# The branch for tokens without a slot, moved from the middle of expert 3 into the routing, with the sums set to zero by GpSimd beforehand

## The chip, the cores and the metric

The kernel runs on one NeuronCore of a Trainium2 chip. The metric is the time of one execution in microseconds of the device (us), the median of several runs. The engines are TensorE (PE for matmuls, PEld for its weight loads), VectorE (DVE), ScalarE (ACT), GpSimd (POOL) and SyncE (SP), which here issues every load of weights.

## The reference, cut to what matters

Two decoder layers on 256 tokens of width 1024, all in float32. The second layer ends in a mixture of experts, and that part is all this study speaks of:

```python
logits = xt @ router_w + router_b            # 256 tokens x 8 experts
top_logit, top_idx = lax.top_k(logits, 2)
gates = softmax(top_logit)
out = swiglu(rows of each expert, w_gate[e], w_up[e], w_down[e])   # 1024 -> 3584 -> 1024
y = segment_sum(out[dest] * gates, tok_sorted)
x = x + gt_f * rmsnorm(y, ffn_post_g)
```

Every token is computed by two of the eight experts. The weights of all eight are read: 3 x 1024 x 3584 float32 numbers for each, 336 transfers of 1 MB in all.

## The kernel before, in words

**Routing.** `to_router` and `first_one` compute the logits, choose two experts for each token (`choose`), rank the tokens within an expert (`ranks`) and put the experts in an order by their counts (`places`, which writes the numbers of the experts to `cnt[1:9]`). The place in that order sets how many slots an expert has: `CAPS = (128, 64) * 4`. Experts at places 0, 2, 4 and 6 have 128 slots and are here called wide, those at 1, 3, 5 and 7 have 64 and are called narrow.

**Weights.** SP reads the expert's number from `cnt` and issues the loads (`load`, line 161), each into a tile of 1 MB called `raw`. The tiles come from pools listed in `turns` (12 tiles) and, for the first loads, from a longer list `first` that also borrows tiles which are needed for something else later: `yp` (1, later the sums `y`), `htp` (2), `xp` and one more. A load waits until what its tile held has been used. For a wide expert ACT and DVE split each tile into `hi` and `lo` (lines 172 and 174) and TensorE multiplies three times (lines 226, 227, 230); for a narrow one TensorE reads the tile itself (lines 1386 and 1438).

**The steps of an expert.** Seven tiles of 512 hidden columns, each with four loads of gate and up weights (`up`) and two of down weights (`down`). One-hot matrices (`onehot`, tile `disp`, line 1180 for the first expert) gather the tokens of an expert into `xT` (matmuls of line 1190, then `fl` by lines 1199 and 1201, then line 1211), and at an expert's end `scatter` adds its output to `y`. For expert 0 ACT copies the product to `y` instead (`fresh`), since `y` holds nothing yet.

**The branch.** A token for which its expert has no slot left is handled in `experts(P)`, a second pass inside `tc.If(over > S)`, called from `overflow`. With the inputs of this study the branch is not taken. `overflow` stands in the pipeline at `cut`, after the first tile of expert 3 (`OVER = 3`). Ahead of it SP issues ten loads (line 1529); then every engine reads `cnt[0]` (line 1531), compares, and jumps over the body (line 1538). `rest` computes `cnt[0]` and the counts beyond the slots three steps into expert 0.

**Order.** `order(...)` switches between regions in which the named engines keep the order of the code and regions in which a scheduler chooses. In the routing all four engines keep the code's order.

Of the kernel before, what the change touches and what calls it, by code (L numbers as in the profile page):

```python
# [17 lines left out]
P = 128  # L18
# [14 lines left out]

HX, OVER = 2, 3
AHEAD = 2
# [48 lines left out]
def kernel(ctx: ExitStack, tc: tile.TileContext, a: dict):  # L84
# [55 lines left out]
    def where(src):  # L140
        return src() if callable(src) else src
# [750 lines left out]
    def warm(n):  # L892

        for _ in range(n):
            T.matmul(psr["warm"], ident, con[:, :512], start=True, stop=True)
# [91 lines left out]
    def moe(l):  # L987
        with ExitStack() as s:
# [8 lines left out]
            some = [htp] * 2 + [lambda: xp.tile([P, UN], F, name="raw", tag="hT2")]  # L997
            first = turns + [yp] + some + [lambda: hTp.tile([P, UN], F, name="raw", tag="hT1")]
            ring.update(n=0, slots=turns, first=first + (turns + [yp] + some) * RND + (turns + some) * RND2)
            gax = ep.tile([P, 2, NE], F, name="gax")  # L1000
# [22 lines left out]
            def places():  # L1023

                room = sqp.tile([P, D], F, name="places", tag="k4", bufs=2)
                match = room[:, :64].rearrange("p (a b) -> p a b", a=NE)
                place = room[:, 128:256].rearrange("p (k a b) -> p k a b", k=2, a=NE)
                number = room[:, 256:320].rearrange("p (a b) -> p a b", a=NE)
                kind = room[:, 64:80].rearrange("p (a b) -> p a b", a=2)
                key = room[:, 512:520]  # L1030
                cps = tr_t("counts").rearrange("p a b -> p (a b)")
                for b in range(2):
                    T.matmul(cps[:, :NE], ones, sel[:, b], start=b == 0, stop=b == 1)
                V.tensor_copy(count, cps[:, :NE])
                V.scalar_tensor_tensor(key, count, float(NE), cn("iota")[:, :NE], op0=OP.mult, op1=OP.add)
                V.tensor_tensor(match, key[:, :, None].to_broadcast(bc), key[:, None, :].to_broadcast(bc), op=OP.is_gt)
                V.tensor_reduce(nth, match, axis=X, op=OP.add)
                V.tensor_tensor(match, cn("nth")[:, :, None].to_broadcast(bc), nth[:, None, :].to_broadcast(bc),
                                op=OP.is_equal)
                V.tensor_tensor(number, match, cn("iota")[:, None, :NE].to_broadcast(bc), op=OP.mult)  # L1040
                V.tensor_reduce(key, number, axis=X, op=OP.add)
                V.tensor_copy(cnt[:, 1:1 + NE], key)

                V.tensor_scalar(kind, sel, -2.0 * S, 2.0 * S, op0=OP.mult, op1=OP.add)
                V.tensor_add(kind, kind, rank)
                for b in range(2):
                    V.tensor_tensor(place[:, b], kind[:, b, None, :].to_broadcast(bc), match, op=OP.mult)
                V.tensor_reduce(at[:, 0:2], place, axis=X, op=OP.add)
# [22 lines left out]

            def rest():

# [6 lines left out]
                V.tensor_copy(cnt[:, 1 + NE:], key)  # L1080
                V.tensor_reduce(m[:, 0:1], key, axis=X, op=OP.max)
                V.tensor_copy(cnt[:, 0:1], m[:, 0:1])
                V.tensor_tensor(beyond, rank, cap[:, None, :].to_broadcast([P, 2, NE]), op=OP.subtract)

            def pipeline(steps, before, late, cut):

                w, later, rest = {}, {}, []
                for i in range(-AHEAD, len(steps)):
# [5 lines left out]
                    if i == len(steps) - 1:  # L1094
                        order(ALL)
                    if i == cut:
                        overflow([src for src, *_ in steps[i + AHEAD - 1:]])
                    if i == -AHEAD:
                        before()
                    if i == 1 - AHEAD:  # L1100
                        more.pop()()
                    for k in range(i + AHEAD - (i == cut), min(i + AHEAD + (i != cut - 1), len(steps))):
                        if steps[k][3]:
# [5 lines left out]
                        else:  # L1109
                            raw = load(steps[k][0])  # L1110
                            w[k] = [part(raw, 0)]
                            rest.append(lambda raw=raw, w=w[k]: w.append(part(raw, 1)))
                    if i == cut:
                        for fn in rest:
                            fn()
                        rest.clear()
                    for fn in later.pop(i, []):
# [24 lines left out]
            def dispatch(es, base):  # L1142
# [77 lines left out]
                def first_one():  # L1220

                    copied, factor = psr["turned"]
                    for g in range(2):
                        copied(g, (A.copy, V.tensor_copy)[g])
                    factor()
                    logits(1)
                    warm(1)
                    choose(1)
                    ranks(1)
                    places()  # L1230
                    warm(1)
# [39 lines left out]

            def scatter(acc, ohT, gs, fresh):

# [6 lines left out]
                def add(b):  # L1280
                    for n in range(2):
                        sp = tr_t("scp").rearrange("p a b -> p (a b)")
                        for j in range(2):
# [4 lines left out]
                            else:  # L1288
                                T.matmul(sp, fr(ohT[:, b, :]), fr(eo[j][:, n, :]), start=j == 0, stop=j == 1)  # L1289
                        if fresh and b == n == 0:  # L1290
                            y.append(yp.tile([P, 2, D], F, name="y", tag="raw"))
                        yy = y[0][:, b, n * 512:(n + 1) * 512]
                        if fresh:
                            A.copy(yy, sp)
                        else:
                            V.tensor_add(yy, yy, sp)

# [42 lines left out]
            def experts(base):  # L1340
# [102 lines left out]
                def spread(e):  # L1443
                    for fn in scatter(st["acc"][e], *st["disp"][e][1](), e == base == 0):
                        yield fn()
# [23 lines left out]
                for n in range(len(tiles) + 1):  # L1469
# [25 lines left out]
                    if n:  # L1495
                        e, i = tiles[n - 1]
                        for u in range(2):
                            follow = []
                            if i == NT - 1 and u == 1 and e < NE - 1:
# [5 lines left out]
                                 small_)  # L1505
                        if (e, i) == (OVER, 0):
                            cut = len(steps)
                steps[-10][2].insert(0, (1, lambda: sums(0)))
                steps[-5][2].insert(0, (2, lambda: sums(1)))
                steps[-30][2].insert(0, (1, ending))  # L1510

                def begin():
                    todo, first_one = start(0)
                    more.append(first_one())
                    steps[0][2].extend([(1, weights), (2, todo[-1]), (3, rest)])

                pipeline(steps, begin, LATE, cut)
                order(ALL)
                finish(st["acc"][NE - 1], *st["disp"][NE - 1][1]())

            def overflow(srcs):

                region.close()
                ready = []
                while len(ready) < min(RAW + RAW2 + 1, len(srcs)):
                    pool = slot()
                    if pool is not rawp3:
                        ready.append(raw_tile(pool))
                        SY.dma_start(ready[-1], where(srcs[len(ready) - 1]))
                n = ring["n"]  # L1530
                over = nc.values_load(cnt[0:1, 0:1], min_val=0, max_val=2 * S,
# [6 lines left out]
                with tc.If(over > S):  # L1538
                    ring.update(slots=[rawp3])
                    experts(P)  # L1540
                spill.clear()
                ring.update(n=n, slots=turns, ready=ready)
                order(ALL if CAPS[OVER] < P else SET)

# [15 lines left out]

            last, gt, y, ht, more = [], [], [], [], []

# [195 lines left out]
```

## Time and profile before

| what | value |
|---|---|
| median of 3 runs | 1348.87 us (1348.35 to 1349.53) |
| the profiled execution's own time | 1351.66 us |
| its span, first to last instruction | 1349.9 us |
| mean granted TensorE clock | 0.99 |
| PE busy | 1308.9 us (97%) |
| DVE, ACT, POOL busy | 61%, 48%, 2% |
| loads of expert weights | 224 + 112 of 1 MB |

The profile divides the span into instructions of each engine, and tells for an engine's idle time which engine or transfer ended it. The experts take the stretch from about 480 us to the end. The profiled execution took 2.79 us longer than the median of the runs; a change in time is worked out within the profiled execution and applied to either.

### The profile page before, as it was taken

To read this page: it belongs to the slowest core of one execution; us is meant where nothing else is said; L and a number is where in the kernel's file an instruction comes from. 1 tells how busy PE (TensorE), PEld (TensorE's weight loads), DVE (VectorE), ACT (ScalarE), POOL (GpSimd) and SP (SyncE) were. 2 spreads that over 40 slices of the span, in tenths; PEclk is the share of its full clock that TensorE was granted. 3 is DMA by queue.
4 is the path that set the end of the run, shared out by engine and by line. 5 is a ranking of instruction groups with operands and counts; after the bars stand their busy time and mean duration, and the time that the engine had idled before them with its cause. 6 is when DMAs were issued, how large, how long until landed. Compare 5 with 4: busy or idle time off the path is not lost. (4 is left out here: it accounts for less than half of the span.)

```text
span 1349.9 us, 18673 instructions
## 1 busy us (share of the span) xinstructions
PE 1308.9 (97%) x6898; PEld 913.6 (68%) x6898; DVE 829.8 (61%) x1260; ACT 645.4 (48%) x961; POOL 27.9 (2%) x48
## 2 busy tenths in 40 slices
PE   6999999999999999999999999899999999999996
PEld 3665588888677567886567886456887556787552
DVE  4796688884688479782139884018986116987201
ACT  4553643533554357673237772027774126775101
POOL 0002000000001100000000000000000000000000
PEclk9999999999999989999999999899999999999998
DMA  9876699886710179999999999899999999999996
GB/s 376 324 276 279 228 396 341 321 319 236 308 65 17 63 314 421 421 420 391 421 421 420 421 421 402 355 421 421 421 420 421 421 420 421 420 421 417 415 396 247
DMA packets 67121, 474.52 MB, mean 352 GB/s; under 512 B 7856, under 2 KB 8272, under 8 KB 10064
## 3 DMA queue, kind: packets, MB, share of 16 engines
q1 hardware_dynamic: 67024, 473.27, 86.6%
q8 instruction: 55, 0.90, 0.3%
q14 instruction: 42, 0.34, 0.1%
HBM read 472.18 MB, written 1.06 MB: 351 GB/s over the span
## 5 line engine op out<-in xcount | busy, mean ns | idle before, releaser
L174 DVE TENSOR_TENSOR lo<-raw,hi 128x1024 fp32r<-128x1024 f32 x442 | 517.6, 1223 | 91.4 <-ACT hi L172 85.4
L172 ACT CAST hi<-raw 128x1024 fp32r<-128x1024 f32 x442 | 445.2, 1050 | 126.0 <-DMA raw<-in_moe_gu_dram 35.9
L1386 PE MATMUL egu<-raw,xT 128*64 128x256 f32 x1792 | 205.4, 384 | 2.0 <-DMA raw<-in_moe_gu_dram 2.0
L226 PE MATMUL egu<-hi,xT 128*128 128x512 f32 x448 | 179.0, 400 | 0.4 <-ACT hi L172 0.4
L227 PE MATMUL egu<-hi,xT 128*128 128x512 f32 x448 | 178.9, 399 | 0.0
L1386 PEld LDWEIGHTS egu<-raw,xT 128*64 128x64 f32 x1792 | 126.0, 138 | 72.6 <-issue 10.6
L230 PE MATMUL egu<-lo,xT 128*128 128x512 f32 x448 | 142.0, 398 | 0.9 <-DVE lo L174 0.9
L1400 DVE TENSOR_TENSOR act<-act,egu 128x512 f32<-128x512 f32 (+1 forms) x56 | 30.8, 550 | 150.8 <-PE egu L1386 150.4
L1438 PE MATMUL eacc<-raw,eT 128*64 128x512 f32 x448 | 102.3, 595 | 0.5 <-ACT eT L1415 0.5
L226 PEld LDWEIGHTS egu<-hi,xT 128*128 128x128 f32 x448 | 84.4, 188 | 25.7 <-ACT hi L172 6.0
L230 PEld LDWEIGHTS egu<-lo,xT 128*128 128x128 f32 x448 | 83.2, 188 | 22.6 <-DVE lo L174 3.8
L227 PEld LDWEIGHTS egu<-hi,xT 128*128 128x128 f32 x448 | 84.4, 188 | 19.8 <-issue 1.8
L1415 ACT COPY eT<-etp 128x256 f32<-128x256 f32 x28 | 10.4, 370 | 164.3 <-PE etp L1405 97.2
L226 PE MATMUL eacc<-hi,eT 128*128 128x512 f32 x224 | 88.8, 397 | 0.0
L227 PE MATMUL eacc<-hi,eT 128*128 128x512 f32 x224 | 88.3, 395 | 0.0
L226 PE MATMUL gu<-hi,hT 128*128 128x512 f32 (+1 forms) x192 | 72.7, 382 | 0.5 <-ACT hT L406 0.5
L227 PE MATMUL gu<-hi,hT 128*128 128x512 f32 (+1 forms) x192 | 71.5, 376 | 0.7 <-DVE hT L407 0.7
L230 PE MATMUL eacc<-lo,eT 128*128 128x512 f32 x224 | 70.7, 397 | 0.0
L226 PE MATMUL proj<-hi,hT 128*128 128x512 f32 x160 | 66.7, 419 | 2.0 <-ACT hT L447 1.0
L1397 ACT ACTIVATE act<-egu 128x512 f32<-128x512 f32 (+1 forms) x56 | 27.4, 490 | 83.9 <-PE egu L1386 82.7
L1438 PEld LDWEIGHTS eacc<-raw,eT 128*64 128x64 f32 x448 | 30.9, 137 | 52.9 <-issue 47.2
L227 PE MATMUL proj<-hi,hT 128*128 128x512 f32 x160 | 64.3, 403 | 0.0
(401 smaller groups left out, 1527.0 us busy)
## 6 DMA issues: line engine op xcount, KB each, us to landing
raw<-in_moe_gu_dram SPq DMA_DIRECT2D x224, 1024.0 KB, 18.0
raw<-in_moe_dn_dram SPq DMA_DIRECT2D x112, 1024.0 KB, 19.6
raw<-in_ada_w_dram SPq DMA_DIRECT2D x48, 1024.0 KB, 6.8
raw<-in_ffn_gu_dram SPq DMA_DIRECT2D x22, 1024.0 KB, 5.0
raw<-in_w_in_dram SPq DMA_DIRECT2D x20, 1024.0 KB, 7.0
raw<-in_ffn_dn_dram SPq DMA_DIRECT2D x11, 1024.0 KB, 5.5
raw<-in_w_out_dram SPq DMA_DIRECT2D x8, 1024.0 KB, 5.9
gate<-gate SPq DMA_DIRECT2D x3, 512.0 KB
```

What stands on the lines that cost most here:

```text
L172: A.copy(fr(hi), raw[:, i * HU:(i + 1) * HU])
L174: V.tensor_sub(fr(lo), raw[:, i * HU:(i + 1) * HU], hi)
L226: T.matmul(ps, fr(xh), fr(hi[:, o:o + n]), start=first, stop=False)
L227: T.matmul(ps, fr(xl), fr(hi[:, o:o + n]), start=False, stop=False)
L230: T.matmul(ps, fr(xh), fr(lo[:, o:o + n]), start=False, stop=last)
L1386: T.matmul(h[m][64 * n:64 * n + 64, :256], xe[:, 0, 4 * u + j, :64], w[:, j * 512 + n * 256:j * 512 + n * 256 + 256], start=u == j == 0, s ...
L1397: A.activation(h["act"], h[0][:, :h["n"]], AF.Silu)
L1400: V.tensor_mul(h["act"], h["act"], h[1][:, :h["n"]])
L1415: A.copy(h["aT"][0][:, :2, :], h["tp"][:, :2, :])
L1438: T.matmul(st["acc"][e][0][64 * n:64 * n + 64, :], h["aT"][0][:, j, 64 * u:64 * u + 64], w[:, j * D + n * 512:j * D + n * 512 + 512], star ...
```

## The change: what it does

The branch moves into the routing: `begin` now runs the rest of the routing itself, calls `overflow` right behind `places`, and only then starts the dispatch of expert 0. `cnt[0]` is computed in `places` by four short DVE instructions. `rest` becomes `without` and, with a copy of `weights`, stands inside the branch. SP issues nine loads ahead of the branch. The tile for `y` is allocated at the start and set to zero by GpSimd (a `memset` of 128x2048), so expert 0 adds to it like all the others; its pool `yp` is no longer in the list `first`.

```diff
-HX, OVER = 2, 3
+HX = 2
...
-            first = turns + [yp] + some + [lambda: hTp.tile([P, UN], F, name="raw", tag="hT1")]
-            ring.update(n=0, slots=turns, first=first + (turns + [yp] + some) * RND + (turns + some) * RND2)
+            first = turns + some + [lambda: hTp.tile([P, UN], F, name="raw", tag="hT1")]
+            ring.update(n=0, slots=turns, first=first + (turns + some) * (RND + RND2))
...
+                cap = room[:, 520:528]
+                V.tensor_scalar(cap, nth, NE / 2 - 0.5, -64.0, op0=OP.is_gt, op1=OP.mult)
+                V.scalar_tensor_tensor(cap, count, S - 64.0, cap, op0=OP.add, op1=OP.add)
+                V.tensor_reduce(m[:, 0:1], cap, axis=X, op=OP.max)
+                V.tensor_copy(cnt[:, 0:1], m[:, 0:1])
...
-                    if i == cut:
-                        overflow([src for src, *_ in steps[i + AHEAD - 1:]])
...
-                        if fresh:
-                            A.copy(yy, sp)
-                        else:
-                            V.tensor_add(yy, yy, sp)
+                        V.tensor_add(yy, yy, sp)
...
                 def begin():
+                    copied, factor = psr["turned"]
...
+                    places()
+                    overflow([src for src, *_ in steps])
+                    psr["warm"] = mm_t("warm")
                     todo, first_one = start(0)
                     more.append(first_one())
-                    steps[0][2].extend([(1, weights), (2, todo[-1]), (3, rest)])
-
-                pipeline(steps, begin, LATE, cut)
+                    steps[0][2].extend([(1, weights), (2, todo[-1])])
...
-                while len(ready) < min(RAW + RAW2 + 1, len(srcs)):
-                    pool = slot()
-                    if pool is not rawp3:
-                        ready.append(raw_tile(pool))
-                        SY.dma_start(ready[-1], where(srcs[len(ready) - 1]))
-                n = ring["n"]
+                while len(ready) < RAW + RAW2 and ring["first"][0] is not rawp3:
+                    ready.append(load(srcs[len(ready)]))
+                held, ring["first"] = ring["first"], None
...
                 with tc.If(over > S):
                     ring.update(slots=[rawp3])
+                    weights()
+                    without()
                     experts(P)
...
-            last, gt, y, ht, more = [], [], [], [], []
+            y0 = yp.tile([P, 2, D], F, name="y", tag="raw")
+            G.memset(y0, 0.0)
+            last, gt, y, ht, more = [], [], [y0], [], []
```

The program's order shows where this lands. On DVE, before, `places` ends with the reduction into `at` (line 1048) and the one-hots of expert 0 (line 1180) stand right behind it:

```order
L1041 TENSOR_REDUCE places<-places 128x8
L1042 CAST cnt<-places 128x8
L1044 TENSOR_SCALAR places<-sel 128x16
L1045 TENSOR_TENSOR places<-places,rank 128x16
L1047 TENSOR_TENSOR places<-places 128x64 x2
L1048 TENSOR_REDUCE at<-places 128x16
L1180 TENSOR_SCALAR disp<-con,at,rx 128x128 x2
```

On DVE now, at the same place, `cnt[0]` is computed (lines 1045 to 1048 of the changed kernel) and the branch (lines 1521 and 1528) closes the stretch:

```order
L1042 CAST cnt<-places 128x8
L1045 TENSOR_SCALAR places<-above 128x8
L1046 SCALAR_TENSOR_TENSOR places<-above,places 128x8
L1047 TENSOR_REDUCE m<-places 128x1
L1048 CAST cnt<-m 128x1
L1050 TENSOR_SCALAR places<-sel 128x16
L1051 TENSOR_TENSOR places<-places,rank 128x16
L1053 TENSOR_TENSOR places<-places 128x64 x2
L1054 TENSOR_REDUCE at<-places 128x16
L1521 TENSOR_LOAD cnt
L1528 COMPARE_AND_BRANCH
```

The one-hots (now line 1178) stand behind the branch's end, so four instructions and a jump came between `places` and them.

On ACT, before, the first work of expert 0 follows the copy of the transposed tokens (`xt`) directly:

```order
L924 COPY xt<-rps 128x4x128
L1201 ACTIVATE fl<-xTp,mod 128x128 x2
L1211 CAST xT<-fl 128x512
L172 CAST hi<-raw 128x1024 x2
L1201 ACTIVATE fl<-xTp,mod 128x128 x2
```

On ACT now, behind the branch, that work (now lines 1199 and 1209) begins with a load of the activation table:

```order
L1528 UNCONDITIONAL_BRANCH
L1199 ACT_TABLE_LOAD
L1199 ACTIVATE fl<-xTp,mod 128x128 x2
L1209 CAST xT<-fl 128x512
L172 CAST hi<-raw 128x1024 x2
```

One table load was added there; before, no table is loaded behind the branch.

On POOL, before, the power for the second half of the tokens (`rx`) follows that for the output norm (`qst`), and then POOL waits at the branch:

```order
L239 TENSOR_TENSOR qst<-nt,half 128x1
L239 TENSOR_TENSOR rx<-nt,half 128x1
L239 TENSOR_TENSOR qst<-nt,half 128x1
L239 TENSOR_TENSOR rx<-nt,half 128x1
L1531 TENSOR_LOAD cnt
```

On POOL now, the memset stands between the two:

```order
L239 TENSOR_TENSOR qst<-nt,half 128x1
L239 TENSOR_TENSOR rx<-nt,half 128x1
L239 TENSOR_TENSOR qst<-nt,half 128x1
L1554 MEMSET y 128x2048
L239 TENSOR_TENSOR rx<-nt,half 128x1
L1521 TENSOR_LOAD cnt
```

The power for `rx` moved behind the memset. The tile `y` lies where ACT's scratch tile `junk` lay until the routing, so the memset in its turn waits for ACT's last square (line 248).

## Rows read from the trace of the kernel before

**Rows 1.** The page: busy time of TensorE, and bytes moved in 40 equal slices.

```profile
PE 1308.9 (97%) x6898; PEld 913.6 (68%) x6898; DVE 829.8 (61%) x1260; ACT 645.4 (48%) x961; POOL 27.9 (2%) x48
...
GB/s 376 324 276 279 228 396 341 321 319 236 308 65 17 63 314 421 421 420 391 421 421 420 421 421 402 355 421 421 421 420 421 421 420 421 420 421 417 415 396 247
```

**Rows 2.** Waits of TensorE: total us, times, longest; the whole execution.

```profile
PE etp L1405 <- DVEq L1538: 4.4, 1, 4.4
...
PE egu L1386 <- DMA raw<-in_moe_gu_dram: 2.0, 1, 2.0
```

**Rows 3.** Chain that ended last, 840 to 875 us: start, us, what.

```profile
849.94 9.24 PE egu L1386 x64
...
862.98 7.06 PE egu L1386 x64
```

**Rows 4.** Instructions of lines 1531 and 1538: count, ns min/median/max, first and last start.

```profile
L1531 DVEq EVENT_SEMAPHORE  x5: 50/50/50, 841.6 to 842.0; - x5
...
L1538 SPq EVENT_SEMAPHORE  x9: 17/17/17, 850.9 to 855.2; - x9
L1538 ACTq EVENT_SEMAPHORE  x2: 17/17/17, 843.1 to 843.2; - x2
...
L1538 DVEq EVENT_SEMAPHORE  x2: 21/21/21, 849.1 to 849.2; - x2
...
L1538 ACTq COMPARE_BRANCH  x1: 50/50/50, 837.7 to 837.7; - x1
...
L1538 DVEq COMPARE_BRANCH  x1: 72/72/72, 842.8 to 842.8; - x1
```

**Rows 5.** Stretches of 5 us around the branch; last three columns: granted clock, DMA share, GB/s.

```profile
850.00:855.00 5.00, 5.00 (x28) 2.86 (x30) 0.00 (x0) 0.37 (x1) 0.00 (x0) 0.57 0.57 229
855.00:860.00 5.00, 5.00 (x46) 2.95 (x44) 0.42 (x1) 0.38 (x1) 0.00 (x0) 1.00 0.58 205
```

**Rows 6.** Timeline of the routing: start, us, instruction, idle before and releaser.

```profile
469.80 0.63 ACT L248 ACTIVATE junk<-x 128x512 f32<-128x512 f32 x1
...
472.34 0.55 POOL L239 TENSOR_TENSOR rx<-nt,half 128x1 f32<-128x1 f32 x1 [4.18 <-DVE nt L238]
...
474.15 0.23 DVE L942 SCALAR_TENSOR_TENSOR lg<-logits,rx,rbias 128x8 f32<-128x8 f32 x1 [1.89 <-PE logits L937]
...
476.87 0.17 DVE L1034 COPY above<-counts 128x8 f32<-128x8 f32 x1 [0.69 <-PE counts L1033]
477.07 0.17 DVE L1035 SCALAR_TENSOR_TENSOR places<-above,con 128x8 f32<-128x8 f32 x1
...
479.77 0.60 DVE L1180 TENSOR_SCALAR disp<-con,at,rx 128x128 f32<-128x128 f32 x2
...
480.17 6.46 PE L1190 MATMUL xTp<-disp,x 128*128 128x128 f32 x32 [1.43 <-DVE disp L1180]
```

**Rows 7.** Transfer of 4 KB while the queues were idle: KB, us to landing.

```profile
con<-in_con_dram SPq DMA_DIRECT2D x1, 4.0 KB, 1.5
```

**Rows 8.** ACT's timeline in expert 0: the table load and what follows it.

```profile
498.86 1.28 ACT L1397 ACT_TABLE_LOAD   x1
500.15 0.60 ACT L1397 ACTIVATE act<-egu 128x512 f32<-128x512 f32 x1
```

**Rows 9.** GpSimd's groups by shape: count, busy us, mean ns of one.

```profile
L1628 POOL TENSOR_TENSOR gw<-gw,con 128x1024 f32<-128x1024 f32 x1 | 3.2, 3219 | 35.5 <-DMA gw<-in_gmlp_w_dram 35.5
...
L513 POOL MEMSET xp<- 128x60 f32 x2 | 0.3, 148 | 0.9 <-ACT sc L287 0.9
...
L110 POOL MEMSET half<- 128x4 f32 x1 | 0.1, 101 | 0.3 <-POOLq L1748 0.3
```

**Rows 10.** SP's issues of loads at the end of expert 0: start, stretch of the issues, count.

```profile
575.92 12.68 SPq L161 DMA_DIRECT2D raw<-in_moe_dn_dram  x2
```

**Rows 11.** Chain that ended last, from 1295 us: start, us, what.

```profile
1300.76 3.61 PE eacc L1438 x16
...
1307.23 16.00 DMA raw<-in_moe_gu_dram
```

More of the change, by code (lines that the diff above doesn't have):

```diff
@@ L1070, in weights, with without @@
                 V.tensor_reduce(at[:, 2:6], place, axis=X, op=OP.add)
-            def rest():
+            def without():
                 room = sqp.tile([P, D], F, name="places", tag="k4", bufs=2)
@@ L1080, in rest, with pipeline @@
                 V.tensor_copy(cnt[:, 1 + NE:], key)
-                V.tensor_reduce(m[:, 0:1], key, axis=X, op=OP.max)
-                V.tensor_copy(cnt[:, 0:1], m[:, 0:1])
                 V.tensor_tensor(beyond, rank, cap[:, None, :].to_broadcast([P, 2, NE]), op=OP.subtract)
-            def pipeline(steps, before, late, cut):
+            def pipeline(steps, before, late):
                 w, later, rest = {}, {}, []
@@ L1101, in pipeline @@
                         more.pop()()
-                    for k in range(i + AHEAD - (i == cut), min(i + AHEAD + (i != cut - 1), len(steps))):
+                    for k in range(i + AHEAD, min(i + AHEAD + 1, len(steps))):
                         if steps[k][3]:
@@ L1112, in pipeline @@
                             rest.append(lambda raw=raw, w=w[k]: w.append(part(raw, 1)))
[L1113 to L1116, printed above, removed]
                     for fn in later.pop(i, []):
@@ L1220, in first_one @@
                 def first_one():
[L1222 to L1230, printed above, removed]
                     warm(1)
@@ L1270, in weigh, with scatter @@
                 V.scalar_tensor_tensor(fr(eo[1][:, n, :]), acc[n], gs, eo[0][:, n, :], op0=OP.mult, op1=OP.subtract)
-            def scatter(acc, ohT, gs, fresh):
+            def scatter(acc, ohT, gs):
                 if len(acc) == 1:
@@ L1289, in add @@
                                 T.matmul(sp, fr(ohT[:, b, :]), fr(eo[j][:, n, :]), start=j == 0, stop=j == 1)
-                        if fresh and b == n == 0:
-                            y.append(yp.tile([P, 2, D], F, name="y", tag="raw"))
                         yy = y[0][:, b, n * 512:(n + 1) * 512]
-                        if fresh:
-                            A.copy(yy, sp)
-                        else:
-                            V.tensor_add(yy, yy, sp)
+                        V.tensor_add(yy, yy, sp)
                 return [lambda: [weigh(acc, gs, eo, n) for n in range(len(acc))], lambda: add(0), lambda: add(1)]
@@ L1443, in spread @@
                 def spread(e):
-                    for fn in scatter(st["acc"][e], *st["disp"][e][1](), e == base == 0):
+                    for fn in scatter(st["acc"][e], *st["disp"][e][1]()):
                         yield fn()
@@ L1505, in experts @@
                                  small_)
-                        if (e, i) == (OVER, 0):
-                            cut = len(steps)
                 steps[-10][2].insert(0, (1, lambda: sums(0)))
@@ L1512, in begin @@
                 def begin():
+                    copied, factor = psr["turned"]
+                    for g in range(2):
+                        copied(g, (A.copy, V.tensor_copy)[g])
+                    factor()
+                    logits(1)
+                    warm(1)
+                    choose(1)
+                    ranks(1)
+                    places()
+                    overflow([src for src, *_ in steps])
+                    psr["warm"] = mm_t("warm")
                     todo, first_one = start(0)
                     more.append(first_one())
-                    steps[0][2].extend([(1, weights), (2, todo[-1]), (3, rest)])
-                pipeline(steps, begin, LATE, cut)
+                    steps[0][2].extend([(1, weights), (2, todo[-1])])
+                pipeline(steps, begin, LATE)
                 order(ALL)
@@ L1539, in overflow @@
                     ring.update(slots=[rawp3])
+                    weights()
+                    without()
                     experts(P)
                 spill.clear()
-                ring.update(n=n, slots=turns, ready=ready)
-                order(ALL if CAPS[OVER] < P else SET)
+                ring.update(n=0, slots=turns, first=held, ready=ready, last=None)
+                order(ALL)
             def free():
```

## Prediction, made before the changed kernel ran

> **What bounds the kernel now.** I read the page first. TensorE is busy for 1308.9 us of the 1349.9 us span, and from the fifteenth slice on the transfers run at 421 GB/s in nearly every slice [rows 1]. So in the experts two resources look full at once, and the question is which of them a delay is passed on by. The next view is that of TensorE's waits. In the whole execution it waits once for expert weights, for 2.0 us, and once at the branch, for 4.4 us [rows 2]. Everywhere else its next operands are there. The chain that ended last says the same: it runs through TensorE's matmuls to 1304.4 us (1300.76 + 3.61) and only then through a transfer of 16.0 us, whose tile those matmuls had just released [rows 11]. The transfers are full because they refill tiles as TensorE gives them back. At the end of expert 0 SP issues two loads 12.7 us apart, where it otherwise issues one every 2.5 us (1 MB at 421 GB/s): no tile was free [rows 10]. From the first product of expert 0 to 1304 us I therefore take TensorE as the pace, and a time lost or gained on it as lost or gained at the end.
>
> Ahead of that, in the routing, the pace is a single chain on DVE: counts, places, one-hots. TensorE sits idle for 1.43 us until the one-hots come [rows 6].
>
> **The change part by part.**
>
> *The stall in expert 3 goes.* TensorE stood still for 4.4 us there [rows 2]. [...] Removed: 4.4 + 2.2 = 6.6 us.
>
> *Transfers at the branch.* SP, once it had jumped, waited from 850.9 to 855.2 us for all the loads issued ahead to land [rows 4], so the queue ran empty: 229 and 205 GB/s in two stretches of 5 us [rows 5], a loss of 2.3 + 2.6 = 4.9 us of transfer time. The same wait comes in the routing, behind nine loads, and costs the same there. I take nothing for it in either place. In expert 0 the loads run ahead of TensorE until SP has to wait for tiles [rows 10], and 4.9 us less lead is covered by that wait. If that cover were gone, up to 4.9 us would be added.
>
> *The branch in the routing.* What stood between `places` and the one-hots was nothing; now DVE goes through these, one after another.
> - Four short instructions for `cnt[0]`, each depending on the one before. Such steps start 0.2 us apart (476.87 and 477.07) [rows 6]: 0.8 us.
> - Waits on semaphores, the load of `cnt[0]` and the comparison. In the branch of before DVE's first wait began at 841.6 us and the comparison at 842.8 us [rows 4]: 1.2 us.
> - The jump. From the comparison to the first instruction behind it, DVE took 6.3 us (842.8 to 849.1) and ACT 5.4 us (837.7 to 843.1) [rows 4], both beside full transfers. No row shows a jump with idle queues. The lower bound is the 1.5 us in which 4 KB landed when the queues were empty [rows 7], the upper one 6.3 us. DVE will jump at about 481.8 us, some two microseconds behind the first load of weights, so the queues are filling: I take ACT's 5.4 us.
> - Two semaphore instructions behind the jump (849.1 to 849.2) [rows 4] and the wait in front of the one-hots: 0.3 us.
>
> Sum: 0.8 + 1.2 + 5.4 + 0.3 = 7.7 us, by which the one-hots of 479.77 us start later, and TensorE's gather with them. Queued behind DVE's jump are the one-hots and the scaling of `xT`; TensorE, ACT and then every product of expert 0 wait for them. TensorE's and ACT's own jumps begin earlier and end inside DVE's.
>
> [...]
>
> *The table load.* ACT now loads its table behind the branch, after it has waited for DVE's part of `fl`, so it lies on the chain to `xT`, to `hi` and to the first product. The one in expert 0 took 1.28 us, and the instruction behind it started with its end (498.86 + 1.28 against 500.15) [rows 8]. I add 1.3 us; below it nothing, if it ran while ACT waits.
>
> [...]
>
> *The memset* can start when ACT's last square ends, at 470.4 us [rows 6]. Two memsets of 4 and 60 elements took 101 and 148 ns, 0.84 ns for each further element [rows 9]: 1.8 us for 2048, done at 472.2 us, ahead of the power that starts at 472.34 us [rows 6]. Nothing is added. The upper bound is the only large GpSimd instruction, 3219 ns for 1024 elements with two inputs [rows 9], or 6.4 us for 2048: the power would end at 470.4 + 6.4 + 0.55 = 477.4 us where DVE needs it at 474.15 us [rows 6], 3.2 us more.
>
> *Small terms.* Expert 0's four copies by ACT become four additions by DVE; the eight short DVE instructions of `rest` leave expert 0. TensorE waits for neither, so nothing. The clock: TensorE idles longer in the routing, and its clock may rise later; I take nothing, and keep for the range as much as it cost behind the old branch, 2.2 us [rows 3]. At the end, the list of tiles is two entries shorter, which moves the late load that waits for its tile forward by one: it is released by the first half of the 3.61 us of matmuls [rows 11] instead of by all of it, 1.8 us earlier, but one load more (2.5 us) then follows: 0.7 us.
>
> **Sum.** 7.7 + 1.3 + 0.7 - 6.6 = 3.1 us more. Within the profiled execution that is 1351.66 to 1354.8 us; it lay 2.8 us above the median of the runs, so the median goes from 1348.87 to about 1352.0 us.
>
> **The rivals.**
>
> *The jump is cheap in the routing.* [...] With 1.5 instead of 5.4 us the sum is -0.8 us, 1348.1 us; with the table load hidden as well -2.1 us, 1346.8 us. For it: between 370 and 475 us almost nothing is transferred, 65, 17 and 63 GB/s [rows 1]. Against it: eight loads are issued before DVE jumps or just after.
>
> *The transfers set the pace (faster).* Then what TensorE loses in the routing is made up from tiles already loaded, and what counts is that the queue no longer runs dry at 855 us: -4.9 us, 1344.0 us. For it: 421 GB/s in nearly all slices [rows 1], and the wait of 2.0 us near the end is one for weights [rows 2]. Against it: the issues 12.7 us apart [rows 10]. It decides from the point at which TensorE's delay at the end of expert 0 is less than what the ring of tiles holds; SP waited for tiles there already, so I see no room.
>
> *The memset is slow.* 3.2 us on top, 1355.2 us. GpSimd's short memsets speak against it, and no long one is in the trace.
>
> [...]
>
> **How the numbers follow.** A change of 0.2% (2.7 us) is about what a measurement of this kernel can tell from none: the bounds are 1346.2 and 1351.6 us. The forecast with jumps between 4.5 and 6.3 us spans 1351.1 to 1352.9 us and gets 0.50, of which 0.12 falls below the upper bound; the drain 0.05; the slow memset 0.10, some of it with the late clock; the cheap jump 0.23; the transfers as the pace 0.12. Faster: 0.12. Same: 0.12 + 0.23 = 0.35. Slower: 0.38 + 0.05 + 0.10 = 0.53. The range for 8 in 10 leaves out the transfers' case and some of the slow memset with the late clock (1355.2 + 2.2): 1346.5 to 1356.0 us.
>
> **What the profile after would show.** Right: on DVE a comparison at about 481.8 us, the one-hots near 487.5 us (479.77 + 7.7) and the first product of line 226 some 9 us later than before (7.7 + 1.3); no wait of TensorE between 840 and 860 us; matmuls of expert 3 all at full clock; SP's queue empty once near 506 us; the issues at the end of expert 0 again far apart. Wrong: one-hots ahead of 484 us (a cheap jump); the pow of `rx` later than 473 us (a slow memset); or a wait of TensorE for weights in experts 1 to 4 that shrinks at the end (the transfers set the pace). A table load that ends before DVE's `fl` would take 1.3 us from the sum.

## The result, and the profile after

The changed kernel takes 1358.39 us (median of four runs, 1356.95 to 1359.93) against 1349.20 us of the kernel before beside it: 1.0064 times as long, 95% interval 1.0052 to 1.0076. Measured again it took 1358.75 us against 1350.16 us, 1.0067 (1.0053 to 1.0081). So the change costs 8.6 to 9.2 us. The forecast was slower by 3.1 us: the sign was right, the size too small by 5.5 to 6.1 us, and the time lies outside of the range.

The page of the changed kernel, to be held against [rows 1]: TensorE's busy time has hardly moved, so what came is waiting.

```profile
PE 1305.9 (96%) x6898; PEld 912.5 (67%) x6898; DVE 833.9 (62%) x1260; ACT 645.3 (48%) x958; POOL 29.5 (2%) x49
```

The waits of TensorE say where. The stop of 4.4 us in expert 3 [rows 2] is gone, 9.9 us stand in the routing, 1.5 us wait for DVE's `sel`, and weights are waited for as little as before (2.0 us). `PEq` is TensorE's sequencer, which carries out the branch.

```profile
PE warm L895 <- PEq L1528: 9.9, 1, 9.9
PE egu L226 <- ACT hi L172: 2.7, 1, 2.7
PE egu L1370 <- DMA raw<-in_moe_gu_dram: 2.0, 2, 1.4
...
PE rank L953 <- DVE sel L949: 1.5, 1, 1.5
```

The timeline of the routing after, the counterpart of [rows 6] (start, us, instruction, idle before and what ended it):

```profile
468.77 0.63 ACT L248 ACTIVATE junk<-x 128x512 f32<-128x512 f32 x1
...
469.53 1.85 DVE L949 TENSOR_SCALAR sel<-above 128x8 f32<-128x8 f32 x1
469.55 1.80 POOL L1554 MEMSET y<- 128x2048 f32 x1 [2.42 <-ACT junk L248]
...
469.61 1.78 DVE L958 TENSOR_SCALAR srx<-above,rx 128x8 f32<-128x8 f32 x1
...
471.44 0.39 PE L953 MATMUL rank<-sel,con 128*128 128x8 f32 x2 [1.53 <-DVE sel L949]
...
477.83 0.17 DVE L1034 COPY above<-counts 128x8 f32<-128x8 f32 x1 [0.69 <-PE counts L1033]
...
481.06 0.29 DVE L1054 TENSOR_REDUCE at<-places 128x16 f32<-128x128 f32 x1
...
488.42 0.60 DVE L1178 TENSOR_SCALAR disp<-con,at,rx 128x128 f32<-128x128 f32 x2 [7.07 <-DVEq L1528]
...
489.50 2.13 PE L1188 MATMUL xTp<-disp,x 128*128 128x128 f32 x9
...
492.81 2.73 PE L1188 MATMUL xTp<-disp,x 128*128 128x128 f32 x23 [1.18 <-issue]
...
494.69 1.28 ACT L1199 ACT_TABLE_LOAD   x1 [24.59 <-DVE fl L1197]
...
498.44 0.80 PE L226 MATMUL egu<-hi,xT 128*128 128x512 f32 x1 [2.68 <-ACT hi L172]
```

Two marks of the kernel before on TensorE, for the shift (first product of expert 0, first products ahead of the old branch, in expert 3):

```profile
487.27 0.50 PE L226 MATMUL egu<-hi,xT 128*128 128x512 f32 x1 [0.42 <-ACT hi L172]
...
818.74 3.46 PE L1386 MATMUL egu<-raw,xT 128*64 128x256 f32 x30
```

And the chain that ended last, after: the same products of expert 3, those of the next tile but one, and the last load that is waited for (of before, [rows 3, 11]).

```profile
829.57 7.06 PE egu L1370 x64
...
866.93 7.06 PE egu L1370 x64
...
1297.27 7.08 PE egu L1370 x64
...
1305.36 1.89 PE eacc L1422 x8
...
1310.45 17.72 DMA raw<-in_moe_gu_dram
```

Read as shifts (how much later the same instruction starts after the change), the two traces give this account. ACT's last square comes 1.03 us earlier (469.80 to 468.77). The first product comes 11.17 us later, so the routing between lost 12.2 us. At expert 3 the shift is 10.83 us: 330 us of work on the experts gave back 0.3. Behind the old place of the branch it is 3.95 us (862.98 to 866.93), so 6.9 us were removed. At the last expert it is 4.60 us (1292.67 to 1297.27), and the spans differ by 5.3 us, 0.7 us more by the end. The 0.6 us between the two tiles come in steps of 0.1 to 0.4 us from expert to expert and have no cause here. Of the 0.7 us, 0.3 lie at the late load (its first product starts at 1323.37 us before and 1328.31 us after), the rest behind the last issue of the output. Together 12.2 - 0.3 - 6.9 + 0.6 + 0.7 = 6.3 us; what separates this from 8.6 us is taken up below.

At the old place the transfers go on at 416 and 418 GB/s, and the granted clock stays at 1.00, where [rows 5] had 0.57, 229 and 205 GB/s:

```profile
850.00:855.00 5.00, 5.00 (x36) 2.38 (x34) 0.42 (x1) 0.00 (x0) 0.00 (x0) 1.00 1.01 416
855.00:860.00 5.00, 5.00 (x44) 2.90 (x42) 0.00 (x0) 0.65 (x2) 0.00 (x0) 1.00 1.01 418
```

The branch itself, line 1528, in the form of [rows 4]: DVE's comparison at 482.2 and its first instruction behind the jump at 488.1 us, 5.9 us. TensorE's comparison and jump take 6.0 us and end at 487.2 us.

```profile
L1528 ACTq EVENT_SEMAPHORE  x2: 17/17/17, 486.3 to 486.4; - x2
...
L1528 DVEq EVENT_SEMAPHORE  x2: 21/21/21, 488.1 to 488.2; - x2
L1528 ACTq COMPARE_BRANCH  x1: 50/50/50, 481.1 to 481.1; - x1
...
L1528 PEldq COMPARE_BRANCH  x1: 6032/6032/6032, 481.2 to 481.2; - x1
...
L1528 DVEq COMPARE_BRANCH  x1: 72/72/72, 482.2 to 482.2; - x1
```

### The profile page after: what moved, and what is told of

The parts are those of the page before. It is cut to its first block, busy times and chain, and to the rows that moved or that the text cites. A ratio compares the mean times of both kernels' runs of the same rounds, so it can differ in the third digit from the quotient of the medians.

```text
span 1355.2 us, 18687 instructions
## 1 busy us (share of the span) xinstructions
PE 1305.9 (96%) x6898; PEld 912.5 (67%) x6898; DVE 833.9 (62%) x1260; ACT 645.3 (48%) x958; POOL 29.5 (2%) x49
## 4 chain that ended last, share of the span: by engine, by line
PE 59%; DMA 3%; issue 1%; DVE 1%; ACT 0%; SPq 0%; DVEq 0%; ACTq 0%
PE egu L1370 13%; PE egu L226 8%; PE egu L230 8%; PE egu L227 8%; PE eacc L1422 6%; PE eacc L226 4%; PE eacc L227 4%; PE eacc L230 4%; DMA raw<-in_moe_gu_dram 3%; PE etp L1389 2%; PE xTp L1188 1%; PE scp L1278 1%; PE scp L1276 1%; SPq L161 0%; PE ohp L1246 0%
```

## The experiments

**Each branch taken out.** The two versions without a branch say what each place costs.

```diff
-                over = nc.values_load(cnt[0:1, 0:1], ...)
...
-                with tc.If(over > S):
...
-                    experts(P)
```

From the kernel before:

> The kernel before without its branch in expert 3 (no load of cnt[0], no comparison, no jump, no pass for tokens without a slot). Theory (there the branch costs what TensorE loses: its stop of 4.4 us and 2.2 to 2.4 us by the lower clock behind it): the time falls by 6.8 us, from 1350.3 to 1343.5 us. Rival 1 (the queue that ran empty at 850 to 860 us was paid for later as well): by up to 4.9 us more, to 1338.6 us. Rival 2 (part of the stop was made up by tiles loaded ahead): by 4 us or less.

1343.46 us against 1350.16 us: 6.7 us (0.9953, 0.9939 to 0.9966), as the theory said. The old branch cost what TensorE lost: by the four traces of the kernel before, a stop of 4.3 to 4.9 us and 1.2 to 2.2 us more for the 64 matmuls behind it. The further 4.9 us that an empty queue might have cost later lie outside of the interval.

From the changed kernel:

> The changed kernel without the branch: no load of cnt[0], no comparison, no jump, no pass for tokens without a slot (with these inputs none has any); the four short instructions for cnt[0], the memset and the loads stay. Theory (the branch costs, at its new place, the 7.1 us of DVE's pause, the 1.2 us of TensorE's stop and the 1.3 us of the table load, and nothing else): 1358.4 - 9.6 = 1348.8 us. Rival 1 (some of it is covered by other work, or the late start of TensorE is made up in the experts): it falls by less, to 1351 us or more. Rival 2 (the branch costs more than its pauses, by the queue that runs empty behind it or by the clock): it falls by 12 us or more, to 1346.5 us or less.

1346.60 us, 11.8 to 12.2 us below the changed kernel (1358.4 to 1358.75). The number is that of rival 2, but neither of its mechanisms is shown. From ACT's square to the first product this version takes 20.7 us, the changed kernel 29.7 to 31.9 us in its three traces, 30.5 us in the mean: 9.8 us. The pauses in the first trace, 7.07 + 1.18 + 1.28 = 9.5 us, account for that. From the first product to the end all four traces take 856.4 to 856.8 us, so the queue that ran empty behind the branch was not paid for there. The other 2 us or so between the medians stay unassigned. The difference between the two versions without a branch, 3.1 us, is what the rest of the change costs: memset, `cnt[0]`, the end.

**The memset.**

```diff
                     factor()
+                    G.memset(y0, 0.0)
                     logits(1)
...
-            G.memset(y0, 0.0)
```

> The changed kernel with GpSimd's memset moved behind its power for rx, some 2 us later in the routing. In the changed kernel two tensor_scalar of DVE (lines 949 and 958) took 1.85 and 1.78 us while the memset ran, against 0.17 and 0.22 us before the change. Theory (the memset holds such DVE instructions up, and at the new place DVE has no tensor_scalar while it runs): both fall back to 0.2 us, the routing from the last square of ACT to the counts gets 2.0 us shorter, and the time falls from 1358.4 to 1356.4 us. Rival 1 (the memset holds every DVE instruction): the 1.7 us move to the choice of experts for the second half of the tokens, and the time stays at 1358.4 us. Rival 2 (the long tensor_scalar have another cause): they stay at 1.8 us.

1356.02 us, 2.4 to 2.7 us less. In the trace the first product comes at 496.42 us, 2.0 us earlier; ACT's square comes 0.5 us earlier, and TensorE's stop in the gather was 0.5 us longer this time (1.64 us):

```profile
469.02 0.17 DVE L949 TENSOR_SCALAR sel<-above 128x8 f32<-128x8 f32 x1
469.10 0.22 DVE L958 TENSOR_SCALAR srx<-above,rx 128x8 f32<-128x8 f32 x1
...
471.38 1.80 POOL L1499 MEMSET y<- 128x2048 f32 x1
472.61 0.23 DVE L942 SCALAR_TENSOR_TENSOR lg<-logits,rx,rbias 128x8 f32<-128x8 f32 x1 [1.89 <-PE logits L937]
472.87 0.22 DVE L946 TENSOR_TENSOR diag<-lg 128x64 f32<-128x64 f32 x1
```

Both tensor_scalar are short again (0.17 and 0.22 us), and DVE's instructions with two tensors run at 0.22 to 0.23 us while the memset runs. So at its early place the memset of 1.80 us held the two tensor_scalar until it ended (1.85 and 1.78 us), at its late place it held no instruction with two tensors, and both rivals fall. Why it holds the ones and not the others, no run shows.

The delay has a second part. In the nine traces with the memset at its early place TensorE's second group of logits took 1.85 us four times and 1.96 to 2.98 us five times; in the eight with the memset later or absent it took 1.85 us each time. From ACT's square to the counts the nine need 9.2 us in the mean, the eight 6.9 us. So the memset costs 2.4 us in the mean, as the times say, and not only the 1.7 us by which `sel` is longer.

**What is jumped over.** Two versions with a shorter body; in the first the pass itself is left out, in the second that for seven of eight experts.

```diff
                 with tc.If(over > S):
-                    ring.update(slots=[rawp3])
+                    V.memset(spill["disp"], 0.0)
+                    T.matmul(spill["mm"][0], ident, con[:, :512], start=True, stop=True)
                     weights()
                     without()
-                    experts(P)
```

> The changed kernel with the body of its branch cut to 27 short instructions (the pass for tokens without a slot is left out; it does not run with these inputs). In the changed kernel DVE stands 7.07 us between the end of places and the one-hots, TensorE stops for 1.2 us in its gather, and ACT loads a table for 1.3 us. Theory (the jump is a fetch of code that lies beyond a long body): the pause on DVE falls to 1.5 us or so (waits, the load of cnt[0] and the comparison took 1.1 us), the stop in the gather goes, and with the table load that the shorter body may spare the time falls by 5.5 + 1.2 + 1.3 = 8 us, from 1358.4 to about 1350.4 us. Rival (the price is that of the branch itself, its waits, register load and merge, whatever it jumps over): the pause stays near 7 us and the time falls by no more than the 1.3 us of the table load, to 1357 us.

1348.93 us against 1350.26 us (0.9992, 0.9983 to 1.0001), 9.5 to 9.8 us less than the changed kernel. DVE went on 0.3 us after its comparison, TensorE 0.3 us:

```profile
L1528 PEldq COMPARE_BRANCH  x1: 228/228/228, 480.8 to 480.8; - x1
...
L1528 PEldq EVENT_SEMAPHORE  x1: 51/51/51, 481.1 to 481.1; - x1
L1528 DVEq COMPARE_BRANCH  x1: 72/72/72, 481.7 to 481.7; - x1
L1528 DVEq EVENT_SEMAPHORE  x1: 21/21/21, 482.0 to 482.0; - x1
```

TensorE's stop in the gather and the table load are gone too (32 matmuls in one group, no load on ACT), so the table load was a matter of what stands in the body. The queues of DMA differ between the two. From 481 to 493 us the changed kernel moves seven packets of instructions:

```profile
q8 instruction: 2, 0.03, 1.1%
q14 instruction: 5, 0.04, 0.8%
```

With the short body no queue of instructions has a packet in that stretch; only data move. The two packets on q8, of 16 KB, fall at 484.5 to 485.0 and 490.0 to 490.5 us: one in TensorE's jump, one just ahead of its stop in the gather (491.63 to 492.81 us).

```diff
-                    for e in range(NE):
+                    for e in range(1):
                         some_ = nc.values_load(cnt[0:1, 1 + NE + e:2 + NE + e], ...)
```

> The changed kernel with the pass for one expert instead of eight in the body of its branch (the pass for the other seven is left out; none runs with these inputs), so that the jump goes over an eighth of the code. With the 27 short instructions alone DVE's pause was 1.2 us, with all eight experts 7.1 us. Theory (a target outside of what the engine holds costs one fetch, however far it lies): the pause stays at 6 to 7 us on every engine whose body still is long (TensorE's has some 440 instructions, DVE's some 55), and the time at 1357 to 1358.5 us; DVE's, with its 55, may fall. Rival (the price grows with what is jumped over): the pause falls to about 1.2 + 5.9/8 = 1.9 us on every engine and the time to 1350 us with the table load kept.

1356.27 us, 2.1 to 2.5 us less. By the program this body has some 210 instructions on DVE, 190 on ACT and 560 matmuls on TensorE; the 55 and 440 of the expectation are too few. DVE jumps in 0.6 us; TensorE and ACT take as long as with eight times the code:

```profile
L1528 DVEq EVENT_SEMAPHORE  x2: 21/21/21, 483.2 to 483.3; - x2
L1528 ACTq EVENT_SEMAPHORE  x2: 17/17/17, 486.7 to 486.8; - x2
...
L1528 ACTq COMPARE_BRANCH  x1: 50/50/50, 481.5 to 481.5; - x1
...
L1528 PEldq COMPARE_BRANCH  x1: 6367/6367/6367, 481.7 to 481.7; - x1
...
L1528 DVEq COMPARE_BRANCH  x1: 72/72/72, 482.6 to 482.6; - x1
...
488.19 0.60 DVE L1178 TENSOR_SCALAR disp<-con,at,rx 128x128 f32<-128x128 f32 x2 [6.41 <-DMA raw<-in_moe_gu_dram]
...
490.20 5.44 PE L1188 MATMUL xTp<-disp,x 128*128 128x128 f32 x32
```

The time hardly falls because a cheap jump on DVE alone does not help: its one-hots still start at 488.19 us, 0.1 us behind TensorE's first semaphore after its jump (488.1 us). The profile names a transfer there; in the next version it names TensorE's sequencer. So the one-hots seem to wait for both jumps, and the later one counts.

Here an engine paid 5.2 us and more or 0.6 us and less, and on TensorE and ACT the price did not grow from one expert's code to eight: 6.4 and 6.0 us on TensorE, 5.2 us both times on ACT. Where the price begins is not settled: ACT's body is shorter than DVE's, and ACT paid. The gather ran here without its stop, though nine loads were ahead.

**What is ahead of the jump.**

```diff
-                while len(ready) < RAW + RAW2 and ring["first"][0] is not rawp3:
+                while len(ready) < 0 and ring["first"][0] is not rawp3:
```

> The changed kernel with none of the nine loads of weights ahead of the branch; SP issues them behind it. Theory (the fetches of code queue behind the data of the loads: they were served 3 to 4 us after the comparison, and took 0.3 to 1.1 us themselves): DVE's pause falls from 7.07 to about 3 us, TensorE's stop of 1.2 us in the gather may stay since loads are under way by then, and the time falls by about 4 us to 1354.4 us; the first load is issued some 4 us later, which nobody waits for, since ACT takes its first tile 12 us after it landed. Rival 1 (the fetch takes its 5 to 6 us whatever the queues hold): the pause stays at 7 us, 1358.4 us. Rival 2 (the later loads are missed): TensorE waits for weights in expert 0 and the time does not fall, or rises by up to 4 us.

1357.54 us, some 1 us less, which the spread of the runs covers. One load still went ahead of the branch, and the jump on DVE took 5.0 us (481.9 to 486.9): rival 1, as it seemed. The one-hots waited for TensorE's jump, and the gather ran without its stop:

```profile
487.19 0.60 DVE L1178 TENSOR_SCALAR disp<-con,at,rx 128x128 f32<-128x128 f32 x2 [6.15 <-PEq L1528]
```

The next version kept that load back too, by giving it the tile that the body uses.

```diff
                 held, ring["first"] = ring["first"], None
+                held.insert(0, held.pop(held.index(rawp3)))
```

> The changed kernel with no load of weights at all ahead of the branch: the first load takes the tile that the body of the branch uses too, so it can't be issued earlier (with the loads merely put behind the branch in the code, one still went ahead of it, and the fetches of all engines started together at 484.2 us, when that load had landed). Theory (a fetch is 8 or 16 KB in one transfer of 0.3 to 1.1 us, and waits behind the data that were issued ahead of it): with idle queues the jump takes 2 us or so instead of 5 to 6, DVE's pause falls from 7.1 to about 3 us, and the time from 1358.7 to about 1354 us. Rival (5 us are the price of a far jump with idle queues too): the pause stays at 6 us, the first load comes some 6 us later, ACT waits for it, and the time stays at 1357 us or more.

1354.84 us (1.0034, 1.0021 to 1.0047), 3.6 to 3.9 us less than the changed kernel. DVE's pause is 4.14 us, of which the jump 3.0 us; TensorE's comparison and jump took 3.8 us instead of 6.0; the gather ran without its stop:

```profile
485.03 0.60 DVE L1178 TENSOR_SCALAR disp<-con,at,rx 128x128 f32<-128x128 f32 x2 [4.14 <-DVEq L1529]
...
486.78 4.51 PE L1188 MATMUL xTp<-disp,x 128*128 128x128 f32 x32
```

So the far jump here has a part that it pays with nearly idle queues as well (a DMA share of 0.05 from 480 to 485 us), 3.0 us on DVE and 3.8 us on TensorE, and a part of 2.9 and 2.2 us that goes when no load is issued ahead of it; with one load of 1 MB ahead DVE paid 2.0 of those 2.9 us, and TensorE's comparison and jump took 6.0 us as with nine.

**The table load.**

```diff
                     overflow([src for src, *_ in steps])
+                    A.activation(tiny, top[:, 0:1], AF.Identity)
```

> The changed kernel with one activation of a single column put right behind the branch on ACT, so that the table is loaded while ACT waits for the gather. Theory (the load of 1.28 us lies on the chain from fl over xT and hi to the first product): the first product starts 1.3 us earlier and the time falls from 1358.4 to 1357.1 us. Rival (another wait ends last at the first product): it stays.

1357.18 us, 1.2 to 1.6 us less. By itself that is little against a spread of 3 us between runs of the changed kernel; together with the rows above, where ACT's first work on `fl` starts when the load ends (494.69 + 1.28 against 495.98 us), it says that the 1.28 us were on the chain, once.

**A version from all of this.** `cnt[0]` comes earlier, DVE makes the one-hots ahead of its jump, the memset and the table load are moved as above, and the two matmuls of line 895 behind TensorE's jump are left out; then the same with no load ahead.

```diff
+                    oh0 = e2.tile([P, 2, P], F, name="disp", tag="disp", bufs=1)
+                    for b in range(2):
+                        V.tensor_scalar(oh0[:, b, :], cn("iota"), at[:, b, 0:1], rx[:, b:b + 1],
+                                        op0=OP.is_equal, op1=OP.mult)
-                    overflow([src for src, *_ in steps])
+                    overflow([src for src, *_ in steps], oh0)
+                    A.activation(tiny, top[:, 0:1], AF.Identity)
```

> A version made from what the runs showed so far: cnt[0] is computed three instructions earlier on DVE, so that TensorE jumps while DVE still works; the one-hots of expert 0 stand ahead of DVE's jump (the pass in the body gets a tile of its own for its one-hots); the table is loaded by a small activation while ACT waits; the memset stands behind the power for rx. Theory: what is left is TensorE's jump, 6.0 to 6.5 us from a comparison at 479.2 us (in the time of the trace of before), so that its gather starts at 485.7 instead of 480.2 us, with the second fetch of 1.2 us behind: 6.7 + 0.7 at the end - 6.7 = 0.7 us above before, 1351 us. Rival (DVE's jump, now behind the one-hots, is as late as before and delays fl): 2 us more, 1353 us.

> That version with no load ahead of the branch. Theory of the fetch that waits behind data: TensorE's jump falls to about 2.5 us, the second fetch may go, and the gather starts some 4 us earlier than with loads ahead, 1347 us, faster than before by 3 us. Rival (a far jump takes 5 us with idle queues too, and the first load is late): 1351 us or more.

1350.84 us (1.0001, 0.9992 to 1.0010) and 1349.55 us (1.0000, 0.9991 to 1.0010) against 1350.25 us. The first is as forecast. The second was to gain 4 us; the medians differ by 1.3 us, and the two ratios do not tell them apart. TensorE's jump was down to 3.8 us already in the first (its comparison, at 478.3 us, came ahead of the first load, at 479.14 us). Both take back all that the change cost, and neither beats the kernel before. In the second TensorE still waits 7.1 us for its jump, from the end of the counts on.

**Runs of the same kernel.**

> The changed kernel once more, unchanged, since the first result is from four runs and its profiled one, 1356.95 us, was the shortest of them. Theory (the pauses at the branch are fixed, and runs differ elsewhere): DVE's pause of 7.1 us, TensorE's stop of 1.2 us, the table load of 1.3 us and the two long tensor_scalar of 1.8 us come again within 0.2 us, and the time is 1356.5 to 1358.5 us, 6 to 9 us above before. Rival (the jump itself differs from run to run by a few us): the pause is another one this time, and with it the time.

1358.75 us. DVE's pause was 7.30, TensorE's stop 1.27, the table load 1.28, the tensor_scalar of `sel` 1.85 us: the pauses came again to 0.2 us. The profiled execution was again the shortest of its runs, so one more execution was traced:

> The changed kernel for one more trace. Its ten timed runs lie between 1356.95 and 1359.94 us, and both profiled ones were the shortest of their runs. Theory (the stretch before the routing differs from run to run by one or two us, as it does between the traces so far, where the same square of ACT starts between 468.3 and 469.8 us): in a longer run this instruction starts later by what the run is longer. Rival (the jump differs): the pause of DVE or the stop of TensorE is longer instead.

This execution took 1358.41 us. The theory was wrong, since ACT's square came earlier (468.33 us); the rival has 0.4 us in TensorE's stop, while DVE's pause was 7.16 us. Most of the time went elsewhere in the routing.

```profile
472.41 2.98 PE L937 MATMUL logits<-wr,xt 128*128 128x8 f32 x16
...
490.13 2.13 PE L1188 MATMUL xTp<-disp,x 128*128 128x128 f32 x9
...
493.88 4.09 PE L1188 MATMUL xTp<-disp,x 128*128 128x128 f32 x23 [1.62 <-issue]
```

The logits took 2.98 us instead of 1.85 to 1.96: the granted clock of 472 to 476 us was 0.61, in the first trace 0.80, and 1.00 from 472 to 474 us before the change. TensorE had just stood idle for 1.53 us behind the memset; it had in the second trace too, where the clock stayed at 1.00, so the idle time alone does not decide it. From the square to the first product it is 31.9 us here, 29.7 and 30.0 us in the other two traces. Three more executions of the kernel before were traced with the same question:

> The kernel before once more, for its trace. Theory (executions differ by the place in the routing at which TensorE's clock falls): in an execution of 1349 to 1350.5 us the gather of expert 0 runs at a granted clock near 1 and takes 3.8 us, as without the branch, and from ACT's last square to the first product it is 15.3 to 16 us; in one of 1351 to 1352 us the gather runs at 0.5 and takes 6.4 us, 17.5 us in all, as in the first trace. Rival (they differ ahead of the routing): 17.5 us in all of them, and the square itself starts at another time.

The other two had the same expectation. They took 1350.90, 1348.89 and 1349.10 us, with 17.3, 17.6 and 16.7 us from the square to the first product and gathers of 6.60, 5.67 and 5.42 us. So the clock of the gather does differ, but by 1 us and not by 2 to 3, and none of the four had the full clock throughout that the version of before without a branch had. With the first trace's 17.5 us the kernel before needs 17.3 us there in the mean, the changed one 30.5 us: 13.2 us more, instead of the 12.2 us of the first pair. They divide into 2.2 us up to the counts (memset), 0.6 for `cnt[0]`, 7.2 for DVE's pause, 0.7 from the one-hots to the gather, and 2.5 from there to the first product (table load and stop). The stop in expert 3 was 4.3 to 4.9 us in the four traces. Of the 8.6 us between the medians that explains 13.2 - 0.3 - 6.9 + 0.6 + 0.7 = 7.3 us, and the mean spans of the three and four traces differ by the same 7.3 us; the last 1.3 us lie within what the traces of one kernel differ by among themselves, and stay unassigned.

## Why the prediction was wrong, by its own steps

| step | forecast, us | shown, us |
|---|---|---|
| stall and lower clock in expert 3 go | -6.6 | -6.7 (without the branch), -6.9 (first pair of traces) |
| four instructions for `cnt[0]` | 0.8 | 0.6 to 0.7 |
| waits, load, jump, semaphores on DVE | 6.9 | 7.07 to 7.30 |
| table load | 1.3 | 1.3 |
| memset | 0 | 2.0 in the first pair, 2.2 to 2.4 in the mean |
| TensorE's two matmuls behind its jump | not seen | 0.7 |
| TensorE's stop in the gather | not seen | 1.2 to 1.6 |
| the end | 0.7 | 0.7, of which 0.3 at the late load |

Five terms out of six were right to 0.4 us; that of the end came out by luck, since the late load that it was worked out from made up less than half of it. **The step that failed is "Nothing is added" for the memset.** Its duration, worked out as 1.8 us from two short ones, was 1.80 us, and it ended ahead of the power as forecast. What was missed is that it runs beside two DVE instructions on the chain from `sel` to the ranks, and holds them until it ends; the power for `rx` then came late because `nt` stood behind them on DVE (472.76 us), not because POOL was busy. The rival of a slow memset had 3.2 us in the right place by the wrong mechanism. The term was made as if an engine that has time costs nobody anything. What the runs showed in its place is 2.2 to 2.4 us.

**The second miss is a term that was not in the sum:** the argument "TensorE's and ACT's own jumps begin earlier and end inside DVE's" is true of the jump (TensorE's last semaphore at 487.6, DVE's first at 488.1 us) but stops there. Two matmuls that stand behind TensorE's jump (line 895, 2.04 us at a granted clock of 0.50) held the gather until 489.50 us, 1.08 us behind the start of the one-hots where it was 0.40 us before. Then the gather itself stopped for 1.2 to 1.6 us after nine matmuls. That TensorE's code behind the target came in a second piece is the author's estimate from the second packet on q8 (16 KB, 490.0 to 490.5 us). With a short body the gather ran through, and with one load or none ahead of the jump; but with one expert's code and nine loads it ran through as well, so data ahead are not the whole cause, and what else decides stays open.

**Two reasons held.** TensorE is the pace from the first product on: 11.17 us at expert 0 were still 10.83 us at expert 3. And the jump costs in the routing about what it cost in expert 3, as the sum has it: on DVE 5.9 us against 6.3 us, with 5.4 us in the sum. Leaving out the empty queue was right as well; the version of before without a branch gained TensorE's loss and not the 4.9 us more. The rival of a cheap jump failed with nine loads ahead; with none it is half true, 3.0 us on DVE against its 1.5, an estimate from a load of 4 KB [rows 7] that no run shows for a jump. The 2.2 us of the lower clock in the sum are 9.24 against 7.06 us [rows 3]; in the four traces of the kernel before they are 1.2 to 2.2 us. A drain behind the table load, which has 0.05 of the chance, no run shows: ACT's first work on `fl` starts as the load ends, at 495.98 us.

## What to carry to other kernels

A branch over a long body cost an engine one far jump, on TensorE the same over one expert's code and over eight: here 5.0 to 6.5 us beside transfers and 2.7 to 3.9 us without, against 0.3 us over the short body (some 20 instructions on DVE, one matmul on TensorE). The runs suggest putting it where the engine that sets the pace is waiting anyway, with no loads issued just ahead, and looking at every engine's first stretch behind it: the latest jump counts, and a stop can follow it. Before work is given to an engine with time to spare, list what the other engines on the chain execute at that moment: here a memset of 1.80 us on GpSimd held two tensor_scalar of DVE for 1.85 and 1.78 us.

## What was not expected of the hardware

- A GpSimd memset of 1.80 us held two DVE tensor_scalar of 128x8 for 1.85 and 1.78 us instead of 0.17 and 0.22, and at its later place left DVE's instructions with two tensors at 0.22 us.
- With nine loads ahead (the changed kernel, the short body, the body for one expert), the price of a jump had two levels and nothing between: 0.6 us or less where the body was short for that engine, 5.2 to 6.5 us where it was not, about the same for one expert's code on TensorE as for eight (6.4 and 6.0 us).
- One load of 1 MB ahead of the jump cost almost as much as nine: 5.0 us against 5.9 us on DVE, with none 3.0 us.
